# A twelfth block by seven products in the MLPs of a two-layer decoder: block 13 joins, and three moves that go with it

## The chip, the cores and the metric

The kernel runs on one core of a Trainium2 chip, as one program. Its metric is the device time in microseconds (us). The engines of the core are TensorE (PE, with its weight loads, PEld), VectorE (DVE), ScalarE (ACT), GpSimd (POOL) and SyncE (SP, which only issues transfers). Each takes its own instructions strictly in the order in which the program wrote them, and they meet through semaphores alone.

## The reference: what is computed

Two decoder layers over 256 tokens of 1024 numbers, all in float32. Each layer is an attention (stick-breaking in the first, native sparse in the second) and an MLP with a residual, and a last norm follows. The change is in the MLP, called twice, and in the last norm:

```
def sqrelu_mlp(x, w1, w2):
    h = jax.nn.relu(x @ w1)
    return (h * h) @ w2

h = h + sqrelu_mlp(rms_norm(h, norm_gain[layer, 1]), mlp_w1[layer], mlp_w2[layer])
...
return rms_norm(h, final_norm)      # x * rsqrt(mean(x * x) + eps) * gain
```

w1 is 1024 x 4096, w2 is 4096 x 1024.

## The kernel before, in words

**Precision.** A float32 product is made of three matmuls (`mm3`): both operands are split into a high part (rounded by a cast) and a low part (the rest), and high x high, high x low and low x high are added up in PSUM. The split is two instructions per operand: a cast on ScalarE makes the high part, a subtraction on VectorE the low part. In the profile wh and wl are the parts of weights, hh and hl those of the hidden numbers, th and tl those of sums of weights.

**Blocks.** The MLP's 4096 hidden numbers are worked off in 16 blocks of 256 (`NFC`), numbered 0 to 15. For block c, `first` (L651 on) computes the hidden numbers in two halves of 128 for all 256 tokens (pu, 16 matmuls each), each into a bank of PSUM, which ScalarE copies to SBUF (mu, L674). `square` (L678 on) adds the two partial results (L689), applies relu and square on ScalarE (L690, L691) and splits them (L695, L696). `half`, called twice per block, multiplies block c - 2 by its piece of w2. That piece is a 2 x 2 arrangement of 128 x 512 tiles, as the hidden numbers are 2 x 2 (two halves of tokens, two halves of hidden numbers). The plain way needs eight products of tiles, which is 24 matmuls.

**Seven products.** Blocks in `FAST` do it with seven products, 21 matmuls, as Strassen's and Winograd's method does. Five products run on sums or differences of tiles. The sums of hidden numbers are made on VectorE (L705 to L707, with a split of 1024 instead of 512 + 256 elements). The two sums of weight tiles are made in one of four buffers (`four0`, `four2` and the two halves of `fours`), into which the block's w2 is loaded: item b by an accumulating transfer that GpSimd issues (L394: the DMA adds what it reads from HBM to what stands in SBUF) and two additions on VectorE (L420, L423), then item a by a second accumulating transfer. They give th and tl (L372, L437). Item a's transfer is queued when b's first addition is done. A buffer is loaded anew when both sums of its last block are split; the count over the four buffers runs on from the first layer to the second.

**Accumulators.** The products go to seven accumulators in PSUM, numbered 1 to 7. Accumulators 2, 3, 4 and 5 end as the four quarters of the result (two halves of tokens t, two halves of columns n), while 1, 6 and 7 hold the products that several quarters share. `gather` combines 1, 6 and 7 (copies on ScalarE, L745 and L746; sums on VectorE, L747 and L748) and adds them to the residual `hres` (`res`, L585), scaled by the norm's factor. Before the change this runs when block 12 is done, while block 15's hidden numbers are computed. Blocks 14 and 15 are multiplied last, quarter by quarter in a given `order`, so that each quarter can be finished while the next is computed; `mid` then calls what follows: in the first layer the turning of the result for the next projection (`to_nsa`: matmuls against the identity, L499), in the second `finish`, the last norm, in which the very last quarter is split into two pieces of 256 columns.

**The order.** Nothing reorders at run time. While the program is written, a planner (`Order`) simulates ScalarE, VectorE and GpSimd with a cost for each operation. Chains of operations (`go`, with a rank) wait for their predecessors in simulated time, and whatever is ready with the lowest rank is written next into its engine's queue. `need` moves the simulated time on to the end of a chain that TensorE depends on. For an accumulating transfer the planner reckons an end (`add_by_queue`, L390 on): the issue plus 1100 and 2700 ns, or behind the transfers before it, plus a fixed mark. Loads are written for SP by `fetch`, in the order of `feed_mlp`, as their buffers come free. `closing` (L1671 on) loads the last norm's gains (gf) and scales them on ScalarE (`whole`, L1677); `gain` (L1712) multiplies a finished quarter by them.

Of the kernel before, what the change touches and what calls it, by code (L numbers as in the profile page):

```python
# [25 lines left out]
NFC = 16  # L26
NGN = 6
EVAC = (0,)
R_GELU, R_SCT, R_SOFT = 0.7, 0.85, 0.9
FAST = ((2, 3, 4, 5, 6, 7, 8, 9, 10, 11, 12),) * 2  # L30
EPS = 1e-5
NEG = -1e30
GELU_C = 2.0 * 0.7978845608028654
# [127 lines left out]
def act(n, f, more=0):  # L161
    return {"A": (195 + 0.835 * n + more, f, False)}


def dve(n, f, more=0, port=False):
    return {"D": (150 + 1.045 * n + more, f, port)}
# [7 lines left out]
def hybrid_kernel(ctx, tc, x, xt, eye, gcols, gfin, wqk, wv, wo0, wkv, wvs, wq, wg, wo1, w1, w2, cw1, cw2, cpos, gate_b, consts, out):  # L174
    nc = tc.nc
# [7 lines left out]
    o = Order()  # L183

    def go(gen, rank=1, lag=LAG):
        return Chain(o, gen, rank, o.now + lag)
# [12 lines left out]
    def B(i, name, dt=F32):  # L199
        return ps.tile([P, 512], dt, tag=f"b{i}", name=name, bufs=1)  # L200
# [26 lines left out]
    def feed_mlp(layer):  # L227
        first = [[feed(w1[layer, c][:, h * H:(h + 1) * H], H) for c in range(2)] for h in range(2)]
        wa, wb = [[first[h][c] for h in range(2)] for c in range(2)], []

        def one(c, h):
            wa[c].append(feed(w1[layer, c][:, h * H:(h + 1) * H], H))

        def two(c, wide):
            s = [w2[layer, c][:, h * H:(h + 1) * H] for h in range(2)]
            fast = c in FAST[layer]
            x = feed(s[0], H, own="x" if fast else False)
            if fast:
                loads.append((s[1], H, 1, "y"))
                ls = [len(loads) - 2, len(loads) - 1]  # L240
                y = item("w", 512, ls[1:])
                quads.append(ls)
            if wide:
                one(c + 2, 1)
            if fast:
                b = item("b", H, ls)
                wb.append([x, y, item("a", H, ls), b])
                pairs[b] = pairs[wb[-1][2]] = x, y
            else:
                wb.append([x, feed(s[1], H)])  # L250

        for c in range(2, NFC):
            wa.append([])
            one(c, 0)
            if not 4 <= c < NFC - 1:
                one(c, 1)
            two(c - 2, 4 <= c < NFC - 1)
        for c in (NFC - 2, NFC - 1):
            two(c, False)
        return wa, wb  # L260
# [22 lines left out]
    class Weights:  # L283
        raws, lands, gone, cur, path, extra, pool, open, four = [], [], 0, -1, 0.0, 0.0, None, False, None

    ws = Weights()
# [103 lines left out]
    def add_by_queue(to, other):  # L390
        w = Waiter()

        def issue():
            nc.gpsimd.dma_start(to, other, accum_op=OP.add)  # L394
            ws.path = max(ws.path, o.t + 1100) + 1450
            ws.extra = max(ws.extra, o.t + 1100) + 2700
            o.at(max(ws.path, ws.extra) + 4300, w.finish)
        return {"G": (1300, issue, False)}, w

    def sums(i, p):  # L400
# [179 lines left out]
    def res(n, t, a, r=None, c0=0, c1=512):  # L580
        hv = hres[t][:, n * 512 + c0:n * 512 + c1]
        if r is None:
            yield dve(512, lambda: nc.vector.tensor_add(hv, a, hv))
        else:
            yield dve(c1 - c0, lambda: nc.vector.scalar_tensor_tensor(hv, a[:, c0:c1], r, hv, op0=OP.mult, op1=OP.add), 60)  # L585
# [11 lines left out]
    def mlp(layer, gi, x_, ch, pt, rs, pus, accs, extra, mid, order, ends, late, ap):  # L597
# [8 lines left out]
        wa, wb = i_m[layer]  # L606
        fast = FAST[layer]
        acc = {}
        banks = {"z": pus[0][0], 1: extra[0], 2: accs[0], 3: accs[2], 4: accs[1], 5: accs[3], 6: extra[1], 7: extra[2]}
        held = []  # L610
        r2, rn = [None, None], [None, None]
        A11, A21, A12, A22, E2, S3, S1, Q, S4 = range(9)

        def term(m, hT, a, w, n, last=False, q=(0, 512)):
            o.need(hT[2][a > 3])
            new = m not in acc
            if new:
                acc[m] = B(banks[m], f"acc{m}")
            a = hT[3][a] * P
            b = cut(W(w), n * 512 + q[0], n * 512 + q[1])  # L620
            mm3(acc[m][:, q[0]:q[1]], (hT[0][:, a:a + P], hT[1][:, a:a + P]), b, new, last)
# [29 lines left out]
        def first(c, st, f, k0, k1):  # L651
            pu, (u, s), chains = st
            if k0 == 0 and c >= 4:
                if free[0] is not None:
                    o.need(free[0])
                pu[f] = B(extra[2] if f and c == NFC - 1 else pus[1][1], "pu")
            for part in range(2):
                for k in range(k0, k1):
                    if c < 2:
                        w, col = W(wa[c][k // 4]), k % 4 * 256 + f * P  # L660
                        if part == 0:
                            o.need(ch[k])
                    else:
                        w, col = W(wa[c][f]), k * P
                    a = cut(w, col, col + P)
                    if part == 0:
                        mm(pu[f], a[0], x_[2][:, k, :, :], k == 0, False)
                    else:
                        mm(pu[f][:, 0:T * P], a[1], x_[0][:, k, :], False, k == NK - 1)
            if c >= 2:  # L670
                gone(wa[c][f])
            if k1 == NK:
                def gen():
                    yield act(512, lambda: nc.scalar.copy(u[:, f, :], pu[f]))  # L674
                chains.append(go(gen(), 0.3))
                free[0] = chains[-1]
# [65 lines left out]
        def gather():  # L742
            g = slot(2, [P, 2, 512], F32, "gp")
            p, v = g[:, 0], g[:, 1]
            yield act(512, lambda: nc.scalar.copy(v, acc[7]))  # L745
            yield act(512, lambda: nc.scalar.copy(p, acc[1]))  # L746
            yield dve(512, lambda: nc.vector.tensor_sub(p, p, acc[6]))  # L747
            yield dve(512, lambda: nc.vector.tensor_add(v, v, p), port=True)  # L748
            yield from res(0, 0, acc[1], r2[0])
            yield from res(1, 0, p, rn[0])  # L750
            yield from res(0, 1, v, r2[1])
            yield from res(1, 1, v, rn[1])

        gathered = None
        for c in range(2, NFC):
            if c == 5:
                scaled = go(scales(), 3)
            st = begin(c)
            apart = 4 <= c < NFC - 1
            first(c, st, 0, 0, NK)  # L760
            if apart:
                half(*held[0], 0)
            first(c, st, 1, 0, NK)
            held.append((c, square(c, st)))
            if not apart:
                half(*held[0], 0)
            half(*held.pop(0), 1)
            if c - 2 == fast[-1]:
                o.need(scaled)
                gathered = go(gather(), 1.5)  # L770
                ws.four = None
                late()

        o.need(gathered)
        for i, (t, n) in enumerate(order):
            m = {(0, 0): 2, (1, 0): 4, (0, 1): 3, (1, 1): 5}[t, n]
            pair = {2: ((A11, 0, 0), (A12, 1, 0)), 4: ((A21, 0, 0), (A22, 1, 0)),
                    5: ((A22, 0, 1), (A21, 1, 1)), 3: ((E2, 0, 1), (S3, 1, 1))}[m]
            for a, h, nn in pair:
                term(m, held[0][1], a, wb[held[0][0]][h], nn)  # L780
            if len(ends[i]) > 1:
                early = go(res(n, t, acc[m], r2[t], *ends[i][0]), 0.19)
            for q in ends[i]:
                if q[0]:
                    o.need(early)
                for a, h, nn in pair:
                    term("z" if q[1] < 512 else m, held[1][1], a, wb[held[1][0]][h], nn, h == 1, q)
                c = [go(res(n, t, acc["z"] if q[1] < 512 else acc[m], r2[t], *q), 0.2)]
                if m == 5:
                    also = go(res(1, 0, acc[m], r2[0]), 0.21)  # L790
                mid(i, t, n, q, c + ([also] if m == 3 else []))
        for h in held:
            gone(wb[h[0]])

# [871 lines left out]
    fin = {}  # L1666
# [4 lines left out]
    def closing():  # L1671
        fin["gf"] = gf = slot(0, [P, D], F32, "gf")
        fin["ys"] = wide_slot(0, [P, T, 2, D], F32, "ys")
        nc.sync.dma_start(gf, gfin.to_broadcast([P, D]))

        def whole():
            yield {"A": (290 + 0.84 * D, lambda: nc.scalar.activation(gf, gf, AF.Copy, scale=float(D) ** 0.5), False)}  # L1677
        go(whole(), 3, 9000)

    def finish(i, t, n, q, c):  # L1680
        gf, ys = fin["gf"], fin["ys"]
# [2 lines left out]
        h = slice(n * 512, (n + 1) * 512)  # L1684
        g = slice((1 - n) * 512, (2 - n) * 512)
        q = slice(n * 512 + q[0], n * 512 + q[1])
        m = q.stop - q.start
# [21 lines left out]
            (nc.scalar if late else nc.sync).dma_start(out[t * P:(t + 1) * P, r], y[:, r])  # L1709

        def gain():
            yield dve(512, lambda: nc.vector.tensor_mul(y[:, h], hres[t][:, h], gf[:, h]), port=True)  # L1712

        def gen():
# [139 lines left out]
```

## Time and profile before

| | |
|---|---|
| time, median of 3 runs | 600.11 us (599.98 to 600.43) |
| the profiled execution's own time | 600.43 us |
| its span, first to last instruction | 598.7 us |
| TensorE busy | 588.6 us, 98% of the span |
| VectorE busy | 515.6 us, 86% |
| ScalarE busy | 433.0 us, 72% |
| GpSimd busy | 94.2 us, 16% |
| mean granted clock of TensorE | 0.997 |

The profile is of one execution. Starts of instructions are in us from the first instruction, and busy is the time in which an engine has an instruction in work. A line's "idle before" is how long its engine had nothing in work before it, with the one that ended the wait. Matmuls are pipelined: one of 512 columns lasts some 390 ns, while the next begins about 230 ns behind it, so stretches, not durations, are summed on TensorE. Most instructions of VectorE and ScalarE also begin a little before the one ahead has ended.

### The profile page before, as it was taken

To read this page: it belongs to the slowest core of one execution; us is meant where nothing else is said; L and a number is where in the kernel's file an instruction comes from. 1 tells how busy PE (TensorE), PEld (TensorE's weight loads), DVE (VectorE), ACT (ScalarE), POOL (GpSimd) and SP (SyncE) were. 2 spreads that over 40 slices of the span, in tenths; PEclk is the share of its full clock that TensorE was granted. 3 is DMA by queue.
4 is the path that set the end of the run, shared out by engine and by line. 5 is a ranking of instruction groups with operands and counts; after the bars stand their busy time and mean duration, and the time that the engine had idled before them with its cause. 6 is when DMAs were issued, how large, how long until landed. Compare 5 with 4: busy or idle time off the path is not lost.

```text
span 598.7 us, 9366 instructions
## 1 busy us (share of the span) xinstructions
PE 588.6 (98%) x3352; PEld 493.1 (82%) x3352; DVE 515.6 (86%) x828; ACT 433.0 (72%) x705; POOL 94.2 (16%) x111
## 2 busy tenths in 40 slices
PE   9999999999999999999999999999999999899995
PEld 6888888888888888888897888777888888688884
DVE  6788997689999999986876899964989999799965
ACT  6767667587988879875925795663878887688863
POOL 0013330001212120000120435130011111111000
PEclk9999999999999999999999999999999999999998
DMA  8982434389987995555553635303699878884502
GB/s 323 401 300 89 133 129 152 108 314 363 244 259 234 248 279 132 153 192 182 176 177 141 249 105 177 107 17 124 197 399 305 229 202 258 240 232 136 158 1 71
DMA packets 37630, 118.78 MB, mean 198 GB/s; under 512 B 4560, under 2 KB 6096, under 8 KB 37584
## 3 DMA queue, kind: packets, MB, share of 16 engines
q1 hardware_dynamic: 31248, 106.88, 50.6%
q0 software_dynamic: 5760, 10.49, 10.7%
q10 hardware_dynamic: 576, 0.82, 0.4%
q8 instruction: 26, 0.43, 0.3%
q14 instruction: 20, 0.16, 0.1%
HBM read 117.12 MB, written 1.05 MB: 197 GB/s over the span
## 4 chain that ended last, share of the span: by engine, by line
PE 86%; ACT 6%; DMA 4%; DVE 2%; issue 1%; POOL 0%; ACTq 0%; POOLq 0%; DVEq 0%
PE acc L487 30%; PE pu L487 26%; PE qk L487 8%; PE pk L487 4%; PE pv L487 4%; PE po L487 3%; PE qp L487 3%; PE z L487 2%; ACT wh L372 2%; DMA fours<-in_w 2%; ACT pe L1341 2%; PE ptp L499 1%; DMA raw<-in_w 1%; PE ph L487 1%; PE pt L499 1%; PE pa L499 1%
## 5 line engine op out<-in xcount | busy, mean ns | idle before, releaser
L387 DVE TENSOR_TENSOR wl<-raw,wh 128x1024 fp32r<-128x1024 f32 x136 | 168.0, 1252 | 7.7 <-ACT wh L372 7.2
L372 ACT CAST wh<-raw 128x1024 fp32r<-128x1024 f32 x136 | 140.7, 1051 | 30.0 <-DMA raw<-in_wq 8.3
L487 PE MATMUL pu<-xn,wh 128*128 128x512 f32 x512 | 128.8, 391 | 0.6 <-ACT mu L674 0.6
L487 PEld LDWEIGHTS pu<-xn,wh 128*128 128x128 f32 x512 | 94.5, 188 | 20.0 <-ACT mu L674 1.4
L487 PEld LDWEIGHTS pu<-xn,wl 128*128 128x128 f32 x512 | 70.9, 190 | 5.7
L487 PE MATMUL pu<-xn,wl 128*128 128x256 f32 x512 | 72.6, 282 | 0.0
L487 PE MATMUL acc<-wh,hh 128*128 128x512 f32 (+1 forms) x146 | 57.1, 391 | 0.0
L487 PE MATMUL acc<-wl,hh 128*128 128x512 f32 (+1 forms) x146 | 56.9, 390 | 0.0
L487 PE MATMUL acc<-wh,hl 128*128 128x512 f32 (+1 forms) x146 | 56.6, 388 | 0.0
L394 POOL DMA_DIRECT2D four<-in_w x22 | 20.5, 932 | 182.5 <-ACT wh L372 61.8
L674 ACT COPY mu<-pu 128x512 f32<-128x512 f32 x64 | 37.3, 582 | 8.7 <-PE pu L487 8.5
L487 PE MATMUL acc<-wh,oT 128*128 128x512 f32 x128 | 43.3, 401 | 0.0
L696 DVE TENSOR_TENSOR hl<-ms,hh 128x1024 fp32r<-128x1024 f32 (+2 forms) x42 | 37.2, 901 | 1.7 <-ACT hh L695 1.5
L487 PE MATMUL acc<-tl,hh 128*128 128x512 f32 x88 | 34.6, 393 | 0.8 <-DVE tl L437 0.8
L487 PE MATMUL acc<-th,hh 128*128 128x512 f32 x88 | 34.6, 394 | 0.3 <-ACT th L372 0.3
L695 ACT CAST hh<-ms 128x1024 fp32r<-128x1024 f32 (+2 forms) x42 | 32.9, 795 | 2.7 <-DVE ms L707 2.3
L487 PE MATMUL acc<-th,hl 128*128 128x512 f32 x88 | 34.2, 389 | 0.0
L487 PE MATMUL pk<-wh,xk 128*128 128x512 f32 (+1 forms) x128 | 32.9, 340 | 0.0
L1341 ACT ACTIVATE pe<-pe,nm 128x256 f32<-128x256 f32 (+1 forms) x64 | 28.4, 447 | 5.6 <-DVE nm L1339 5.6
L487 PE MATMUL qk<-xa,wh 128*128 128x512 f32 x128 | 32.5, 395 | 0.0
L487 PEld LDWEIGHTS acc<-wh,hl 128*128 128x128 f32 x146 | 27.4, 188 | 5.8
L437 DVE TENSOR_TENSOR tl<-four,th 128x1024 fp32r<-128x1024 f32 x24 | 29.1, 1218 | 3.4 <-ACT th L372 3.3
(230 smaller groups left out, 1189.0 us busy)
## 6 DMA issues: line engine op xcount, KB each, us to landing
raw<-in_w SPq DMA_DIRECT2D x84, 512.0 KB, 5.5
four<-in_w SPq DMA_DIRECT2D x24, 512.0 KB, 7.8
fours<-in_w SPq DMA_DIRECT2D x20, 512.0 KB, 7.6
raw<-in_wqk SPq DMA_DIRECT2D x16, 512.0 KB, 6.2
raw<-in_wo SPq DMA_DIRECT2D x16, 512.0 KB, 3.9
four<-in_w POOLq DMA_DIRECT2D x22, 256.0 KB, 5.7
fours<-in_w POOLq DMA_DIRECT2D x18, 256.0 KB, 7.1
raw<-in_wkv SPq DMA_DIRECT2D x8, 512.0 KB, 4.0
```

The lines of the kernel that those rows point to most:

```text
L372: k = {"A": (195 + 0.835 * m, lambda: nc.scalar.copy(a, b), False), "D": (200 + 0.49 * m, lambda: nc.vector.tensor_copy(a, b), True)}
L387: yield {"D": (150 + 1.045 * m, lambda: nc.vector.tensor_sub(lo, raw, f32(hi)), True)}
L394: nc.gpsimd.dma_start(to, other, accum_op=OP.add)
L437: yield {"D": (150 + 1.045 * H, lambda: nc.vector.tensor_sub(lo2, both, f32(hi2)), True)}
L487: nc.tensor.matmul(o_, a, b, start=first, stop=last, skip_group_check=True)
L499: nc.tensor.transpose(o_, a, i)
L674: yield act(512, lambda: nc.scalar.copy(u[:, f, :], pu[f]))
L695: yield act((b - a) * P, lambda: nc.scalar.copy(hh[:, into], flat[:, q]))
L696: yield dve((b - a) * P, lambda: nc.vector.tensor_sub(hl[:, into], flat[:, q], f32(hh[:, into])), port=True)
L1341: act(n, lambda: nc.scalar.activation(d, d, AF.Exp, bias=nm[:, i:i + 1], scale=-1.0, accum_out=rs[:, t, hd, b:b + 1]), 150)]
```

## The change

Block 13 joins the blocks with seven products, in both layers (`FAST` is now blocks 2 to 13 of 0 to 15), which gives each layer twelve such blocks and 24 sums of weight tiles. Blocks 4 to 15 now all have their first `half` put between the two halves of their hidden numbers; before, block 15's two hidden halves ran one behind the other, with the second in the bank of accumulator 7, which was free by then. The load of the second half of block 15's first-layer weights comes behind block 13's.

The accumulators 1, 6 and 7 are now complete only behind block 13, which is the last block ahead of the closing order. So `gather` starts there, with rank 0.25 in place of 1.5 and accumulator 1 added to the residual first. The products of block 14 for the first two quarters come before anything of block 15 (`pair_of`). The first two quarters' later steps wait for `gather`; `need(gathered)` stands before the third quarter's later steps, and in the last round before its last pieces, one of which takes accumulator 1's bank in the second layer.

The planner's fixed mark for the end of an accumulating transfer goes from 4300 to 5800 ns. `closing` is called with `gather`, one block later; its scaling has rank 1 and a lag of 4000 ns in place of rank 3 and 9000, and `gain` now waits for it in the plan.

```diff
-FAST = ((2, 3, 4, 5, 6, 7, 8, 9, 10, 11, 12),) * 2
+FAST = (tuple(range(2, 14)),) * 2
...
             one(c, 0)
-            if not 4 <= c < NFC - 1:
+            if c < 4:
                 one(c, 1)
-            two(c - 2, 4 <= c < NFC - 1)
+            two(c - 2, c >= 4)
...
-            o.at(max(ws.path, ws.extra) + 4300, w.finish)
+            o.at(max(ws.path, ws.extra) + 5800, w.finish)
...
-                pu[f] = B(extra[2] if f and c == NFC - 1 else pus[1][1], "pu")
+                pu[f] = B(pus[1][1], "pu")
...
             p, v = g[:, 0], g[:, 1]
-            yield act(512, lambda: nc.scalar.copy(v, acc[7]))
+            yield from res(0, 0, acc[1], r2[0])
             yield act(512, lambda: nc.scalar.copy(p, acc[1]))
-            yield dve(512, lambda: nc.vector.tensor_sub(p, p, acc[6]))
+            yield [dve(512, lambda: nc.vector.tensor_sub(p, p, acc[6])), act(512, lambda: nc.scalar.copy(v, acc[7]))]
             yield dve(512, lambda: nc.vector.tensor_add(v, v, p), port=True)
-            yield from res(0, 0, acc[1], r2[0])
             yield from res(1, 0, p, rn[0])
...
-            apart = 4 <= c < NFC - 1
+            apart = c >= 4
...
-                gathered = go(gather(), 1.5)
+                gathered = go(gather(), 0.25)
...
-        o.need(gathered)
+        pairs_of = {2: ((A11, 0, 0), (A12, 1, 0)), 4: ((A21, 0, 0), (A22, 1, 0)),
+                    5: ((A22, 0, 1), (A21, 1, 1)), 3: ((E2, 0, 1), (S3, 1, 1))}
+        m_of = [{(0, 0): 2, (1, 0): 4, (0, 1): 3, (1, 1): 5}[x] for x in order]
+
+        def pair_of(j):
+            for a, h, nn in pairs_of[m_of[j]]:
+                term(m_of[j], held[0][1], a, wb[held[0][0]][h], nn)
+
         for i, (t, n) in enumerate(order):
-            m = {(0, 0): 2, (1, 0): 4, (0, 1): 3, (1, 1): 5}[t, n]
-            pair = {2: ((A11, 0, 0), (A12, 1, 0)), 4: ((A21, 0, 0), (A22, 1, 0)),
-                    5: ((A22, 0, 1), (A21, 1, 1)), 3: ((E2, 0, 1), (S3, 1, 1))}[m]
-            for a, h, nn in pair:
-                term(m, held[0][1], a, wb[held[0][0]][h], nn)
+            m = m_of[i]
+            pair = pairs_of[m]
+            if i != 1:
+                pair_of(i)
+            if i == 0:
+                pair_of(1)
+            if i == 3:
+                o.need(gathered)
...
-                mid(i, t, n, q, c + ([also] if m == 3 else []))
+                if i == 2:
+                    o.need(gathered)
+                mid(i, t, n, q, c + ([also] if m == 3 else []) + ([gathered] if i < 2 else []))
...
-        go(whole(), 3, 9000)
+        fin["whole"] = go(whole(), 1, 4000)
...
         def gain():
+            yield fin["whole"]
             yield dve(512, lambda: nc.vector.tensor_mul(y[:, h], hres[t][:, h], gf[:, h]), port=True)
```

## The prediction

> **What bounds the kernel now.** I read the page first, for what is busy.
>
> ```profile
> span 598.7 us, 9366 instructions
> ...
> PE 588.6 (98%) x3352; PEld 493.1 (82%) x3352; DVE 515.6 (86%) x828; ACT 433.0 (72%) x705; POOL 94.2 (16%) x111
> ```
>
> TensorE sets the time: 588.6 of 598.7 us. So a matmul fewer is time saved, as long as nobody makes TensorE wait. Whether somebody does is read by stage. The second view is a table of stretches (length, then busy time and count of PE, weight loads, DVE, ACT, POOL; then clock, DMA share, GB/s). It covers blocks 4 to 13 of the second MLP: five blocks, one, another, three.
>
> ```profile
> 453.01:504.58 51.57, 51.57 (x266) 44.14 (x265) 50.17 (x71) 44.15 (x58) 8.74 (x10) 1.00 0.83 242
> 504.58:517.40 12.82, 11.10 (x55) 8.60 (x53) 9.44 (x12) 7.96 (x11) 1.75 (x2) 1.00 0.83 211
> ...
> 528.04:559.09 31.05, 31.05 (x161) 26.59 (x160) 30.95 (x41) 26.40 (x35) 3.52 (x4) 1.00 0.59 172
> ```
>
> Two things are to be seen. A block takes 10.35 us (31.05/3) with TensorE full, and one block takes 12.82: 2.47 us are lost there. And VectorE is nearly as full as TensorE, 30.95 of 31.05: work that the change adds to VectorE has little room beside the matmuls.
>
> Third, the timelines about the lost 2.47 us (start, length, instruction, idle time before and who ended it): ScalarE, then TensorE, then GpSimd.
>
> ```profile
> 512.97 1.05 ACT L372 CAST th<-four 128x1024 fp32r<-128x1024 f32 x1 [3.55 <-DMA four<-in_w]
> ```
>
> ```profile
> 514.07 0.51 PE L487 MATMUL acc<-th,hh 128*128 128x512 f32 x1 [0.34 <-ACT th L372]
> 515.33 0.51 PE L487 MATMUL acc<-tl,hh 128*128 128x512 f32 x1 [0.76 <-DVE tl L437]
> ...
> 517.40 2.12 PE L487 MATMUL pu<-xn,wh 128*128 128x512 f32 x8 [0.63 <-ACT mu L674]
> ```
>
> ```profile
> 502.26 0.88 POOL L394 DMA_DIRECT2D fours<-in_w  x1 [12.32 <-DVE hl L696]
> 502.95 1.09 POOL L394 DMA_DIRECT2D four<-in_w  x1
> ```
>
> A cast of summed weights (th) stands in ScalarE's queue 3.55 us for an accumulating transfer into "four". GpSimd issued it at 502.95, directly behind another one that had kept its queue waiting. It landed just before 512.97, some 10 us later. All transfers of this kind together, with who waited for them:
>
> ```profile
> who waited for it (us, times):
>   ACT th L372: 6.1, 4
> ...
> DMA to landing us min/median/max: 4.1/6.2/10.8
> ```
>
> **The change, part by part.** *Block 13 by seven products.* The chain of waits lists TensorE's stretches in order (start, length, count). First a plain block (both halves), then the two halves of a fast one; then, for use below, the end of the first MLP.
>
> ```profile
> 141.79 5.47 PE acc L487 x24
> ...
> 150.02 2.07 PE acc L487 x9
> ...
> 154.85 2.75 PE acc L487 x12
> ...
> 266.88 13.63 PE acc L487 x60
> 280.51 0.87 PE pt L499 x8
> ```
>
> 24 matmuls take 5.47 us, 21 take 2.07 + 2.75 = 4.82. Block 13 changes from the one to the other in each of two layers: 2 x 0.65 = **1.30 us less on TensorE**, which is the path.
>
> What it adds elsewhere is read from VectorE's timeline, a fast block's rows first, a plain block's after.
>
> ```profile
> 548.44 1.22 DVE L437 TENSOR_TENSOR tl<-four,th 128x1024 fp32r<-128x1024 f32 x1
> 549.58 1.22 DVE L387 TENSOR_TENSOR wl<-four,wh 128x1024 fp32r<-128x1024 f32 x1
> 550.71 0.41 DVE L705 TENSOR_TENSOR ms<-ms 128x256 f32<-128x256 f32 x1
> 551.05 0.68 DVE L420 TENSOR_TENSOR four<-four 128x512 f32<-128x512 f32 x1
> 551.65 0.28 DVE L706 TENSOR_TENSOR ms<-ms 128x128 f32<-128x128 f32 x1
> ...
> 553.19 0.68 DVE L387 TENSOR_TENSOR wl<-four,wh 128x512 fp32r<-128x512 f32 x1
> 553.91 0.69 DVE L423 TENSOR_TENSOR four<-four 128x512 f32<-128x512 f32 x1
> 554.51 1.22 DVE L696 TENSOR_TENSOR hl<-ms,hh 128x1024 fp32r<-128x1024 f32 x1
> ...
> 558.52 2.35 DVE L387 TENSOR_TENSOR wl<-raw,wh 128x1024 fp32r<-128x1024 f32 x2
> 560.79 0.42 DVE L710 TENSOR_TENSOR ms<-ms 128x256 f32<-128x256 f32 x1
> 561.13 1.22 DVE L437 TENSOR_TENSOR tl<-four,th 128x1024 fp32r<-128x1024 f32 x1
> 562.27 1.02 DVE L696 TENSOR_TENSOR hl<-ms,hh 128x512 fp32r<-128x512 f32 x2
> ```
>
> A fast block's weights take 1.22 + 0.68 (wl), 0.68 + 0.69 (sums) and 2 x 1.22 (tl) = 5.71 us, its hidden part 0.41 + 2 x 0.28 (L706, and L707 like it) + 1.22 = 2.19: together 7.90. A plain block takes 2.35 + 0.42 + 1.02 = 3.79. So VectorE gets 4.1 us more per layer. What hides it is how far ahead VectorE is by then: the tl at 561.13 ends at 562.35, and TensorE first uses it here:
>
> ```profile
> 568.14 0.39 PE L487 MATMUL acc<-tl,hh 128*128 128x512 f32 x1
> ```
>
> That is 5.8 us early, and it is block 12's last. Block 13's sums take the next place in the line, due one block of 10.35 us later. A fast block needs 7.90, plus 0.68 for the hidden sum and 2 x 1.22 for the next first-layer weights: 11.0 us of VectorE in 10.35, so the lead shrinks by about 0.7 to 5. Cost on the path: nothing; if that lead were gone, up to 2 x 4.1 us. In the second layer VectorE also gets back what it stood idle in the stall (12.82 - 9.44 = 3.4 us).
>
> ScalarE's added casts:
>
> ```profile
> 549.76 1.04 ACT L372 CAST th<-four 128x1024 fp32r<-128x1024 f32 x1
> 550.70 0.61 ACT L372 CAST wh<-four 128x512 fp32r<-128x512 f32 x1
> ```
>
> Two th casts more, and one whole cast (taken at 1.04 too) becomes 0.61: + 1.65 us per layer. ScalarE has 31.05 - 26.40 = 4.65 us free in three blocks, so this is hidden. GpSimd gets two more issues per layer of about 1 us each and is 16% busy, but its queue is in order: an issue that waits for a load holds the one behind it, as at 502.26.
>
> *Order of loads and banks for block 15.* The load of the second half of its first-layer weights moves behind block 13's two loads in SP's queue. SP was through with its loads here, when it issued the next thing, the last norm's factors:
>
> ```profile
> 561.33 0.38 SPq L1674 DMA_DIRECT2D gf<-in_gfin  x1
> ```
>
> Block 15 begins only at 559.09 + 10.35 = 569.4, so this costs nothing. The factors are still queued behind the last load, wherever the text now calls for them: they are there long before the first product with them. That product now waits for the scaled factors by name: nothing. Block 15's second hidden bank is now the common one. Its copy to SBUF hides under the 2.07 us half that is put between.
>
> *Accumulators combined behind block 13.* The combining (two copies, six VectorE steps) ran under block 15; here its first copy in the second layer, and its last step:
>
> ```profile
> 569.47 0.59 ACT L745 COPY gp<-acc 128x512 f32<-128x512 f32 x1 [2.16 <-PE acc L487]
> ```
>
> ```profile
> 578.43 0.75 DVE L585 SCALAR_TENSOR_TENSOR hres<-gp,rn,hres 128x512 f32<-128x512 f32 x1
> ```
>
> It took 9.7 us, at low rank between other work. The new place begins after block 13's last matmul. In the first layer the turning matmuls (280.51) need all of it: between lie six groups of six matmuls, 36 x 13.63/60 = 8.2 us. Its bare steps are, by these rows, 0.59 for a copy, 2 x 0.69 for the sums and 4 x 0.75, about 5.0 us; with a higher rank they give way less. So it costs between 0 and 9.7 - 8.2 = 1.5 us. In the second layer the squares and gains of the first two outputs now wait for it and pile up near the end: again 0 to 1.5. There is room for both:
>
> ```profile
> 579.20:591.60 12.40, 12.37 (x60) 10.22 (x58) 7.57 (x15) 4.09 (x11) 0.56 (x1) 1.00 0.00 0
> 271.10:280.51 9.41, 9.41 (x44) 7.76 (x43) 5.11 (x7) 2.76 (x5) 1.19 (x3) 1.00 0.73 233
> ```
>
> VectorE is idle for 4.8 and 4.3 us there, as much as the combining needs. I take + 0.2 in each layer, near the low end.
>
> *Later order behind accumulating transfers.* The planner's mark for the end of such a transfer moves 1.5 us back: it reckoned 1.1 + 2.7 + 4.3 = 8.1 us from the issue, now 9.6. The longest took 10.8. This adds no instruction; it puts other ready casts and subtractions ahead of th and tl. In the stall, order alone can save only what stood behind the th: the 0.63 us wait for mu and something of the rest. The 0.34 + 0.76 us are the late landing itself. But the order, GpSimd's queue and the buffers' rotation (22 sums before, 24 now, over four buffers, so that the second layer starts in another one) all shift, and the stall was a coincidence in one of the nine blocks shown. Bounds: 0 (it comes again) to 2.47 saved; a cost too, below. I take **2.0 saved**, nearer to the rows of the eight full blocks.
>
> By the Trainium skill, "DMA: Bandwidth & Descriptors", section on the anatomy of one DMA on the SWDGE path, a GpSimd-issued DMA takes about 2.0 us plus its bytes over 436 GB/s: 2.6 us for 256 KB, an estimate. By that the old mark was already late enough, and a later one can gain nothing: 599.2, the first rival's time. The trace disagrees on the size, 4.1 to 10.8.
>
> *Sum.* The profiled execution took 600.43 us (span 598.7 and 1.7 around it), the highest of three and 0.32 above their median of 600.11. 600.43 - 1.30 - 2.0 + 0.4 = 597.5, and 597.2 against the median.
>
> **Rivals.** *The stall stays.* The late landing comes from GpSimd's queue order and a slow load, which the change doesn't mend. Then 600.11 - 1.30 + 0.4 = 599.2. For it: 1.10 us of the stall is the landing. Against it: everything in the second layer shifts.
>
> *The combining comes too late.* With 1.5 us in each layer in place of 0.2: 597.2 - 0.4 + 3.0 = 599.8. For it: it took 9.7 us before. Against: its rank, and VectorE's idle time.
>
> *The later mark makes the transfers themselves late, and it is slower.* The second sum's transfer is only put in GpSimd's queue once the first sum is made, and that is now planned up to 1.5 us later, so it may also fall behind the next block's. ScalarE stood waiting for a transfer at four places. If each lands 1.5 us later, that is at most 6.0 us; with half of it taken up by the lead and the old stall kept, 600.11 - 1.30 + 3.0 = 601.8. It decides where a landing comes later than 1.05 + 1.22 = 2.3 us (th, tl) before its matmul. Against it: the other sums have more lead, like the 5.8 us above.
>
> **How the numbers follow.** The forecast has 0.58, the stall that stays 0.20, the late combining 0.10, the late transfers 0.12. 0.2% is 1.2 us, about what a measurement of this kernel can tell from no change: faster is below 598.9, slower above 601.3. The forecast is faster but for 0.01; a stall that stays in part is faster (0.07) or the same (0.13); late combining is mostly the same (0.07), with 0.02 faster and 0.01 slower; late transfers are slower (0.10) or the same (0.02). So faster 0.66, same 0.23, slower 0.11. The range goes from 595.8 (all 2.47 us saved, no cost at the ends, 596.3, and half a microsecond of scatter in other waits) to 601.2, which leaves out most of the last rival.
>
> **What would show it.** TensorE with 3346 matmuls, six fewer. Blocks 12 and 13 at 10.35 us each, with no wait of TensorE for tl. Accumulators' first VectorE step right behind block 13, the last one before the transposes in layer 0, with no idle time ahead of those. No TensorE gap over 0.3 us in blocks 4 to 13 of layer 1, and ScalarE's wait for accumulating transfers well below 6.1 us. The forecast is wrong if such a gap is there again, if VectorE's lead over TensorE is used up before block 13, or if the tail behind the last matmul grows from its 7 us.

## The result, and the profile after

The kernel went from 600.05 us (median of four executions, 599.39 to 600.43) to **596.51 us** (four executions, 596.19 to 597.56): a ratio of 0.9945, with a 95% interval of 0.9928 to 0.9962. That is 3.54 us less. The profiled execution of the changed kernel is its slowest, 597.56 us, as that of the kernel before was (600.43), so the two traces differ by 2.87 us and not by 3.54.

The page of the changed kernel, busy time by engine:

```profile
span 595.8 us, 9379 instructions
...
PE 586.3 (98%) x3346; PEld 492.2 (83%) x3346; DVE 522.5 (88%) x838; ACT 437.5 (73%) x707; POOL 98.0 (16%) x115
```

Six matmuls fewer, 6.9 us more busy time on VectorE, 4.5 more on ScalarE, and TensorE still has 98% of the span. The table of stretches for the second MLP of the changed kernel (length, then busy time and count of PE, weight loads, DVE, ACT, POOL; clock, DMA share, GB/s): eight blocks from block 4 on, then one, then two.

```profile
452.08:534.84 82.76, 82.76 (x426) 70.85 (x425) 80.16 (x110) 70.84 (x91) 14.02 (x16) 1.00 0.85 250
534.84:546.22 11.38, 10.36 (x54) 8.53 (x52) 9.02 (x12) 7.53 (x11) 1.74 (x2) 1.00 0.75 182
546.22:567.23 21.01, 21.01 (x107) 17.98 (x108) 20.87 (x28) 18.19 (x23) 1.73 (x2) 1.00 0.45 126
```

Eight blocks take 82.76/8 = 10.35 us each, as full blocks did before. One still stalls: 11.38 in place of 12.82. ScalarE's and TensorE's timelines of the changed kernel show it as the old stall, smaller and three blocks later, a cast of th that waits for an accumulating transfer:

```profile
540.85 1.05 ACT L372 CAST th<-four 128x1024 fp32r<-128x1024 f32 x1 [2.61 <-DMA four<-in_w]
...
545.60 0.57 ACT L674 COPY mu<-pu 128x512 f32<-128x512 f32 x1
```

```profile
546.22 2.14 PE L487 MATMUL pu<-xn,wh 128*128 128x512 f32 x8 [1.02 <-ACT mu L674]
```

What is late for TensorE is no longer th. It is mu, the copy that empties a bank: it stands behind this th and four other casts in ScalarE's queue. All accumulating transfers of the changed kernel (before: 6.1 us, four times; 4.1/6.2/10.8):

```profile
who waited for it (us, times):
  ACT th L372: 3.4, 2
...
DMA to landing us min/median/max: 4.1/6.5/10.3
```

The transfers land no sooner than before. They are waited for less.

Cut at the same five places, by the starts of TensorE's instructions in each profiled execution, the spans differ as follows (us). "A" is blocks 4 to 14 of the first MLP, "B" goes from its block 15 to block 4 of the second MLP, "C" is blocks 4 to 14 of the second, "D" goes on to the last matmul's end, "E" is what lies behind. Eleven full blocks take 113.81. The rows below the first two are experiments. One execution of e5_changed took 729.75 us at a granted clock of 0.752 and is left out of its figures.

| kernel | A | B | C | D | E |
|---|---|---|---|---|---|
| before | 114.07 | 191.69 | 116.42 | 22.30 | 7.09 |
| after | 113.83 | 190.99 | 115.15 | 21.58 | 7.13 |
| e1_no_block13 | 113.81 | 193.16 | 113.81 | 22.29 | 7.09 |
| e2_mark_4300 | 113.84 | 190.99 | 116.33 | 21.58 | 7.13 |
| e3_before_mark_5800 | 113.87 | 192.37 | 113.81 | 22.29 | 7.09 |
| e4_gather_late | 113.88 | 191.03 | 113.81 | 21.59 | 7.13 |
| e5_changed | 113.81 | 191.14 | 113.81 | 21.58 | 7.13 |
| e6_before_mark_second | 113.83 | 191.69 | 113.81 | 22.29 | 7.09 |
| e7_block13_first_only | 113.83 | 191.00 | 113.81 | 22.29 | 6.63 |
| e8_before_b_later | 113.84 | 191.73 | 113.81 | 22.29 | 6.93 |
| e9_gains_gpsimd | 113.88 | 191.01 | 113.83 | 21.59 | 6.66 |
| e10_mark_2800_second | 113.83 | 191.03 | 116.40 | 21.59 | 7.14 |
| e11_gains_and_b_later | 113.90 | 191.32 | 113.86 | 21.58 | 6.66 |
| e12_changed_again | 113.87 | 191.03 | 113.83 | 21.58 | 7.13 |

Of the 2.87 us between the two traces, B and D give 0.70 + 0.72 = 1.42, C gives 1.27, A gives 0.24 (a small wait less in the first MLP), and E takes 0.04.

### The profile page after: what moved, and what is told of

It reads as the page before. It is cut to its first block, busy times and chain, and to the rows that moved or that the text cites. A ratio compares the mean times of both kernels' runs of the same rounds, so it can differ in the third digit from the quotient of the medians.

```text
span 595.8 us, 9379 instructions
## 1 busy us (share of the span) xinstructions
PE 586.3 (98%) x3346; PEld 492.2 (83%) x3346; DVE 522.5 (88%) x838; ACT 437.5 (73%) x707; POOL 98.0 (16%) x115
## 4 chain that ended last, share of the span: by engine, by line
PE 86%; DMA 5%; ACT 5%; DVE 2%; issue 1%; SPq 0%; ACTq 0%; POOL 0%; POOLq 0%
PE acc L487 31%; PE pu L487 27%; PE qk L487 8%; PE pk L487 4%; PE po L487 3%; PE qp L487 3%; PE pv L487 3%; PE z L487 2%; DMA four<-in_w 2%; ACT wh L372 2%; ACT pe L1352 2%; DMA fours<-in_w 2%; PE ptp L499 1%; DMA rv<-in_wv 1%; PE ph L487 1%; PE pt L499 1%
## 5 line engine op out<-in xcount | busy, mean ns | idle before, releaser
L387 DVE TENSOR_TENSOR wl<-raw,wh 128x1024 fp32r<-128x1024 f32 x132 | 163.3, 1254 | 10.2 <-ACT wh L372 9.8
L372 ACT CAST wh<-raw 128x1024 fp32r<-128x1024 f32 x132 | 135.6, 1051 | 27.7 <-DMA raw<-in_wq 8.8
L487 PE MATMUL acc<-wh,hh 128*128 128x512 f32 (+1 forms) x136 | 53.3, 392 | 0.0
L487 PE MATMUL acc<-wl,hh 128*128 128x512 f32 (+1 forms) x136 | 53.1, 390 | 0.0
L487 PE MATMUL acc<-wh,hl 128*128 128x512 f32 (+1 forms) x136 | 52.7, 388 | 0.0
L394 POOL DMA_DIRECT2D fours<-in_w x24 | 21.5, 895 | 144.0 <-DVE ms L707 57.5
L394 POOL DMA_DIRECT2D four<-in_w x20 | 19.2, 961 | 148.1 <-DMA four<-in_w 61.0
L487 PE MATMUL acc<-th,hh 128*128 128x512 f32 x96 | 37.7, 392 | 0.0
L487 PE MATMUL acc<-tl,hh 128*128 128x512 f32 x96 | 37.6, 392 | 0.0
L487 PE MATMUL acc<-th,hl 128*128 128x512 f32 x96 | 37.3, 389 | 0.0
```

Of the source, the lines that this page charges most:

```text
L372: k = {"A": (195 + 0.835 * m, lambda: nc.scalar.copy(a, b), False), "D": (200 + 0.49 * m, lambda: nc.vector.tensor_copy(a, b), True)}
L387: yield {"D": (150 + 1.045 * m, lambda: nc.vector.tensor_sub(lo, raw, f32(hi)), True)}
L487: nc.tensor.matmul(o_, a, b, start=first, stop=last, skip_group_check=True)
```

## The experiments

The theory was the prediction's: 1.3 us from the matmuls, the rest from the stall, by the later mark. The rivals were that something else removes the stall (the rotation of the buffers, or chance), and that the combining costs more or less than it was given. The experiments ran in three later series, on the chips numbered 12 and 5; for the first pair no chip is on record. In these series the kernel before has a median of 598.2 to 598.3, with executions from 597.3 to 601.5. So each is read against the runs of the kernel before beside it, and its stages in the table above.

**Block 13 as before, all else changed (e1_no_block13)**

```diff
-FAST = (tuple(range(2, 14)),) * 2
+FAST = (tuple(range(2, 13)),) * 2
```

> The changed kernel with block 13 by eight products again (11 blocks per layer as before); the later mark, the rank of the combining and the reordered last products stay. My theory (block 13 gives its matmuls, the later mark gives the rest by easing the stall of the second layer): 1.3 us over the changed kernel, about 597.8, and the block that lost 2.47 us before loses about 1 us at most. Rival (the stall moved because the four buffers start elsewhere in the second layer, the mark does nothing): the buffers start as before, so the stall is back and the time is 599 to 600.

Measured: 599.56 us, a ratio of 1.0017 (1.0006 to 1.0027) to the kernel before. In the table D is 0.71 above the changed kernel's, as 3 matmuls should be, but B is 2.17 above. The surplus is new waits, in stages that the edit doesn't mean. ScalarE's timeline of e1_no_block13 at the end of the first MLP, then TensorE's:

```profile
272.00 1.05 ACT L372 CAST wh<-raw 128x1024 fp32r<-128x1024 f32 x1 [2.16 <-PE acc L487]
272.96 0.63 ACT L690 ACTIVATE ms<-ms 128x512 f32<-128x512 f32 x1
```

```profile
274.95 0.50 PE L487 MATMUL acc<-wh,hh 128*128 128x512 f32 x1 [0.27 <-ACT hh L695]
...
380.13 0.66 PE L499 MATMUL ptp<-ident,pe 128*128 128x128 f32 x4 [0.41 <-ACT pT L1405]
```

A cast for the next stage stands ahead of block 15's relu and waits 2.16 us for a buffer; and in the attention behind, a turning matmul waits. These two gaps are 0.68 us of the 1.47 by which B exceeds that of the kernel before; the rest was not traced. The planner's order is one for the whole program: an edit in one stage moves others, and the medians of such kernels are not the price of the edit. What this run does show is in C: with the old rotation of 22 sums and the mark at 5800 there is no stall in this trace, 113.81. So the time lies in the rival's 599 to 600, but not by the rival's mechanism.

**The changed kernel with the old mark (e2_mark_4300), and the reverse (e3_before_mark_5800)**

```diff
-            o.at(max(ws.path, ws.extra) + 5800, w.finish)
+            o.at(max(ws.path, ws.extra) + 4300, w.finish)
```

> The changed kernel with the planner's old mark of 4300. Theory: the stall comes back in the second layer, 598.3 to 599.0 (2 us over the changed kernel). Rival (buffers): no different from the changed kernel, 596.2 to 597.

> The kernel before with the mark at 5800 and nothing else. Theory: the mark alone gives about 2 us, 598, with ScalarE's 3.55 us wait in front of a th cast at least halved. Rival (buffers, or chance of the whole order): within 0.5 us of the kernel before, 599.6 to 600.4, the wait as long.

Measured: e2_mark_4300 596.95 us, ratio 0.9974 (0.9961 to 0.9988); e3_before_mark_5800 598.50, ratio 0.9997 (0.9986 to 1.0008). By the medians the mark does next to nothing, on either kernel, as the rival had it for e2_mark_4300. By the one trace of each it does all: C is 116.33 with the new rotation and the old mark, 113.81 with the old rotation and the new mark. ScalarE's timeline of e2_mark_4300:

```profile
510.95 1.05 ACT L372 CAST th<-four 128x1024 fp32r<-128x1024 f32 x1 [2.23 <-DMA four<-in_w]
...
539.09 1.05 ACT L372 CAST th<-four 128x1024 fp32r<-128x1024 f32 x1 [1.33 <-DMA four<-in_w]
...
551.24 1.05 ACT L372 CAST th<-four 128x1024 fp32r<-128x1024 f32 x1 [2.96 <-DMA four<-in_w]
```

Both are right. The profiled execution of e2_mark_4300 is its slowest, 599.34; ten of its other eleven are between 596.18 and 597.30. The stall comes in some executions and not in others.

The changed kernel itself shows this. The runs after, e5_changed and e12_changed_again are one program, with the same instructions in the same order on VectorE, ScalarE and GpSimd, and C is 115.15, 113.81 and 113.83. GpSimd's two accumulating transfers in front of the stall, in the changed kernel and then in e12_changed_again, each pair with its time to landing:

```profile
529.76 0.88 POOL L394 DMA_DIRECT2D fours<-in_w  x1 [7.38 <-DVE tl L437]
530.46 1.07 POOL L394 DMA_DIRECT2D four<-in_w  x1
...
DMA to landing us min/median/max: 8.4/9.4/10.3
```

```profile
528.90 0.87 POOL L394 DMA_DIRECT2D fours<-in_w  x1 [7.43 <-DVE ms L707]
529.60 1.07 POOL L394 DMA_DIRECT2D four<-in_w  x1
...
DMA to landing us min/median/max: 5.1/6.7/8.3
```

The order is the same, the landings are not: the load in front of the first transfer took 9.45 us in the one and 8.16 in the other, the second transfer 10.3 and 8.3, and ScalarE waited 2.61 us for it or not at all.

And e3_before_mark_5800 also has waits of its own in B, 192.37 against 191.69 (its turning matmul at 379.96 us waits 0.42 us, like that of e1_no_block13), which hide what the mark saves. That needed an edit that leaves the first layer alone.

**The mark in the second MLP alone, in the kernel before (e6_before_mark_second)**

```diff
-            o.at(max(ws.path, ws.extra) + 4300, w.finish)
+            o.at(max(ws.path, ws.extra) + ws.mark, w.finish)
...
-        ws.tp = ap
+        ws.tp, ws.mark = ap, (4300, 5800)[layer]
```

> The kernel before with the later mark in the second MLP only, so that everything up to there is written in the old order. Theory (the mark takes the stall away): no gap of TensorE over 0.3 us in the second MLP, the times lie close together, and the median is that of the stall-free executions, 597.3 to 598.0 on a chip whose floor is 597.3. Rival (the mark does nothing, the order of the attention cost e3 0.7 us by itself): a spread as wide as the kernel before's and its median within 0.3 us.

Measured: 598.18 us (597.51 to 598.90 in 12 executions), a ratio of 0.9989 (0.9976 to 1.0002). The kernel before beside it: 598.34, 597.29 to 601.45. The stretch C of e6_before_mark_second:

```profile
453.28:567.09 113.81, 113.81 (x584) 97.45 (x583) 110.33 (x146) 95.62 (x123) 15.83 (x18) 1.00 0.77 219
```

TensorE is busy for the whole of it, and B, D and E are those of the kernel before. In these 12 executions the upper end of the times, which reached 601.45, is gone, as the theory had it. The median moves by 0.16 only, as the rival had it, and the interval of the ratio includes 1.

**The mark still earlier, in the changed kernel's second MLP (e10_mark_2800_second)**

```diff
-            o.at(max(ws.path, ws.extra) + 5800, w.finish)
+            o.at(max(ws.path, ws.extra) + ws.mark, w.finish)
...
-        ws.tp = ap
+        ws.tp, ws.mark = ap, (5800, 2800)[layer]
```

> The changed kernel with the mark moved the other way, to 2800, in the second MLP only. Theory (an early mark puts casts ahead of their transfers): longer and more waits of ScalarE in front of th casts than with 4300 (2.2, 1.3 and 3.0 us in e2's profile), blocks 4 to 14 of the second MLP above 115.5 us in place of 113.8, and a median over 597.5. Rival (the mark only shuffles the order): no worse than the changed kernel, 596.3 to 597.

Measured: 598.72 us (597.58 to 601.69), against 596.65 (596.01 to 597.03) for the changed kernel on the same chip, e12_changed_again: 2.07 us slower. The waits for accumulating transfers in the second MLP, and three of the casts in ScalarE's timeline of e10_mark_2800_second:

```profile
who waited for it (us, times):
  ACT th L372: 7.6, 7
...
DMA to landing us min/median/max: 4.2/6.0/8.9
```

```profile
486.55 1.05 ACT L372 CAST th<-fours 128x1024 fp32r<-128x1024 f32 x1 [2.35 <-DMA fours<-in_w]
...
518.00 1.05 ACT L372 CAST th<-fours 128x1024 fp32r<-128x1024 f32 x1 [3.00 <-DMA fours<-in_w]
...
538.62 1.05 ACT L372 CAST th<-four 128x1024 fp32r<-128x1024 f32 x1 [1.02 <-DMA four<-in_w]
```

With the rotation and everything else kept, an earlier mark gives seven waits in place of none to two in the other traces of the changed kernel, although no transfer here took more than 8.9 us. So the mark sets how often th stands ahead of its transfer, and that is not a matter of buffers.

**The first transfer later in GpSimd's queue, in the kernel before (e8_before_b_later).** In the old stall two accumulating transfers stood behind each other in GpSimd's queue. The loads into that buffer, which SP issued from 489.88 on, in the kernel before:

```profile
489.88 0.87 SPq L320 DMA_DIRECT2D fours<-in_w  x2
...
DMA to landing us min/median/max: 8.9/10.1/11.3
```

The second one, issued at 490.3, landed 11.3 us later, at 501.6. Only then could GpSimd issue item b's transfer (502.26), and item a's, for which th was to wait, came behind it (502.95). The profile's row names a VectorE instruction as the releaser of that wait, which ended within 0.1 us of the load. But the issue comes 0.66 to 0.67 us behind the landing of that block's load in four traces (this one, e6_before_mark_second, and the pairs of the changed kernel and of e12_changed_again above), and 0.18 to 0.58 behind the instruction that is named: it is the load that was waited for. The edit lets item b's chain start later in the plan, in the second layer, with the mark at 4300:

```diff
-... got[min(p, cuts - 1)] + (1500 if kind in "ab" else 0))
+... got[min(p, cuts - 1)] + (1500 if kind == "a" else ws.hold if kind == "b" else 0))
...
-        ws.tp = ap
+        ws.tp, ws.hold = ap, (1500, 5000)[layer]
```

> The kernel before with the first accumulating transfer of a block (b) put into GpSimd's queue 3.5 us later in the plan, in the second MLP only, so that it no longer stands ahead of the second transfer (a) of the block before while its load is still under way. Theory of the queue (a late load of b holds up a): no idle time of ScalarE over 1 us in front of a th cast, and 597.3 to 598.0 on a chip whose floor is 597.3. Rival (the transfer itself is slow, wherever it stands): waits and times as in the kernel before.

Measured: 597.88 us (597.19 to 598.80), a ratio of 0.9986 (0.9973 to 0.9999). GpSimd's timeline of e8_before_b_later at the same place, then its stretch C:

```profile
497.97 0.88 POOL L394 DMA_DIRECT2D four<-in_w  x1 [8.01 <-ACT mu L674]
498.51 1.25 POOL L394 DMA_DIRECT2D fours<-in_w  x1
```

```profile
453.00:566.81 113.81, 113.81 (x584) 97.44 (x583) 110.90 (x146) 95.59 (x123) 15.88 (x18) 1.00 0.77 220
```

Item a's transfer now stands first, 0.54 us ahead of b's, and the stall is gone from the trace, with the old mark: ScalarE waits for no accumulating transfer in the second MLP. But the trace doesn't show that the order did it. The load that took 11.3 us before took 7.9 here (issued at 489.36, landed at 497.26), so that in the old order too item a's transfer would have gone out near 498.5, an estimate from GpSimd's second row, in place of 502.95. It is the same in e6_before_mark_second. There the load took 7.7 us, and the two transfers stand in the old order:

```profile
499.18 0.88 POOL L394 DMA_DIRECT2D fours<-in_w  x1 [9.37 <-DVE ms L707]
499.87 1.09 POOL L394 DMA_DIRECT2D four<-in_w  x1
```

So no trace shows what either edit does when a load is late. That they help is read from the times: none of the 24 executions of the two took more than 598.90 us, while 8 of the 31 of the kernel before beside them took 599.29 or more. That those 8 had the stall is inferred, as none of them has a trace. Nor is it settled whether GpSimd's order or ScalarE's is what helps: both edits put other casts first in ScalarE's queue as well, and no kernel here changes one queue alone.

**The combining at its old rank (e4_gather_late)**

```diff
-                gathered = go(gather(), 0.25)
+                gathered = go(gather(), 1.5)
```

> The changed kernel with the combining at the old rank of 1.5. My theory: VectorE has room, so 596.5 to 597.2, and the turning matmuls in the first layer wait 0 to 0.5 us. Rival (late combining): it takes 9.7 us as before, the turning matmuls wait 1.5 us and the last layer's end grows by as much: 598.5 to 599.5.

Measured: 597.01 us, a ratio of 0.9969 (0.9957 to 0.9982); B 191.03, D 21.59 and E 7.13 are the changed kernel's to 0.04. The rank costs nothing in either layer's stretches. The median can't be told from the changed kernel's on that chip, 596.65 in another series (e12_changed_again).

**Block 13 in the first layer alone (e7_block13_first_only)**

```diff
-FAST = (tuple(range(2, 14)),) * 2
+FAST = (tuple(range(2, 14)), tuple(range(2, 13)))
```

> The changed kernel as it is, timed with the next three beside the same kernel before. Where the accounts agree: 1.3 us under the kernel before from the matmuls. Theory that the stall is a matter of chance from one execution to the next: where the kernel before has it in few executions (median near its lowest), the whole gain is 1.3 to 1.8 us; where it has it in most, 3 to 3.6 us.

> The changed kernel with block 13 by eight products in the second MLP only; the first MLP and the attention stay as changed. Theory (three matmuls are worth 0.65 us per layer and nothing else hangs on them): 0.65 us over the changed kernel. Rival (VectorE bears the added sums only just, they cost TensorE something): less than 0.4 us over it, or under it.

Measured on one chip: the changed kernel again (e5_changed) 596.60, ratio 0.9961 (0.9947 to 0.9975); e7_block13_first_only 596.85, ratio 0.9965 (0.9951 to 0.9978). Block 13's second-layer part was expected to be worth 0.65 us and is worth 0.25. The table says why: against e5_changed D is 0.71 longer, as three matmuls are, but E is 0.50 shorter. So in the second layer the later combining costs half a microsecond behind the last matmul. VectorE's timeline at the end of the changed kernel, whose last matmul ends at 588.65; then TensorE's last one into accz:

```profile
587.72 0.68 DVE L1724 TENSOR_TENSOR ys<-hres,gf 128x512 f32<-128x512 f32 x1
588.32 0.48 DVE L585 SCALAR_TENSOR_TENSOR hres<-accz,r,hres 128x256 f32<-128x256 f32 x1
588.71 0.48 DVE L585 SCALAR_TENSOR_TENSOR hres<-acc,r,hres 128x256 f32<-128x256 f32 x1
```

```profile
587.52 0.28 PE L487 MATMUL accz<-wh,hl 128*128 128x256 f32 x1
```

accz is complete at 587.80, but a product with the norm's gains, put off by the combining, stands ahead in VectorE's queue: the residual of accz starts 0.52 us late. In the kernel before it started 0.04 behind its matmul.

**Those products on GpSimd (e9_gains_gpsimd), with the later b as well (e11_gains_and_b_later), and the changed kernel beside them (e12_changed_again)**

```diff
-            yield dve(512, lambda: nc.vector.tensor_mul(y[:, h], hres[t][:, h], gf[:, h]), port=True)
+            yield pool(512, lambda: nc.gpsimd.tensor_mul(y[:, h], hres[t][:, h], gf[:, h]))
```

> The changed kernel with the products of the finished quarters and the last norm's gains on GpSimd in place of VectorE. Theory (at the end VectorE makes a gain product of 0.68 us ahead of the next to last residual piece, because the combining came late, and the chain behind the last matmul starts 0.5 us later): that piece starts 0.8 us before the last matmul's end as in the kernel before, the last store lands 0.5 us sooner behind the last matmul (5.55 against 6.05 us), and the time is 0.3 to 0.5 us under the changed kernel. Rival (the end hangs on ScalarE's squares or on the stores): no different.

> The changed kernel with both: the gains on GpSimd and the first accumulating transfer of a block put 3.5 us later into GpSimd's queue in the second MLP. Theory: 0.5 us from the end and what is left of the stall (about 0.2 us in the mean, the spread's upper end): 595.6 to 596.2, and no execution over 597. Rival (with the later mark the queue no longer matters): the same as the gains alone.

> The changed kernel once more, as the measure of the three beside it on the same chip: 596.3 to 597.0 where the kernel before has its median near 598.3, 596.5 where that is at 600.

Measured: e9_gains_gpsimd 596.12 us, ratio 0.9962 (0.9947 to 0.9977); e11_gains_and_b_later 596.29, ratio 0.9963 (0.9949 to 0.9977); e12_changed_again 596.65, ratio 0.9971 (0.9960 to 0.9981). VectorE at the end of e9_gains_gpsimd (last matmul's end 587.44), then GpSimd:

```profile
586.32 0.20 DVE L1737 TENSOR_SCALAR ssq<-ssq 128x1 f32<-128x1 f32 x1
586.63 0.48 DVE L585 SCALAR_TENSOR_TENSOR hres<-accz,r,hres 128x256 f32<-128x256 f32 x1
587.48 0.48 DVE L585 SCALAR_TENSOR_TENSOR hres<-acc,r,hres 128x256 f32<-128x256 f32 x1 [0.36 <-PE acc L487]
```

```profile
581.38 1.67 POOL L1724 TENSOR_TENSOR ys<-hres,gf 128x512 f32<-128x512 f32 x1 [20.89 <-DVE hres L585]
583.99 2.70 POOL L1724 TENSOR_TENSOR ys<-hres,gf 128x512 f32<-128x512 f32 x2 [0.94 <-DVE hres L585]
```

The residual of accz starts 0.04 us behind its matmul again, E falls from 7.13 to 6.66, and the median by 0.53, though the intervals of the two ratios overlap. The last store lands 5.58 us behind the last matmul, in the changed kernel 6.05. These three products take twice as long on GpSimd, and no instruction waits for them. The later b adds nothing on top: with the later mark no effect of it is to be seen. These two are the fastest kernels of the study.

## Why the prediction was right, and where it was not

**The matmuls: right.** 3346 of them. Predicted 1.30 us less; B and D give 0.70 + 0.72, and between the experiments D differs by 0.70 to 0.72 wherever block 13's second-layer part does.

**VectorE and ScalarE beside it: right.** The lengths of VectorE's instructions add up to 8.0 us more than before, those of ScalarE's to 3.7, near the 2 x 4.1 and 2 x 1.65 of the prediction. No wait for tl or th of block 13 is in the trace. VectorE's lead is seen in its timeline and TensorE's, in the second layer of the changed kernel:

```profile
570.71 1.22 DVE L437 TENSOR_TENSOR tl<-fours,th 128x1024 fp32r<-128x1024 f32 x1
```

```profile
576.28 0.39 PE L487 MATMUL acc<-tl,hh 128*128 128x512 f32 x1
```

It ends at 571.93 and is used 4.35 us later; predicted was "about 5", from 5.8.

**The combining: the sum was near, its parts were not.** Predicted 0.2 in each layer. In the first layer it costs nothing. VectorE's timeline of the changed kernel, its first and last step there, and the chain of waits with the turning matmuls, which wait for nobody:

```profile
271.44 0.74 DVE L585 SCALAR_TENSOR_TENSOR hres<-acc,r,hres 128x512 f32<-128x512 f32 x1
...
277.73 0.74 DVE L585 SCALAR_TENSOR_TENSOR hres<-gp,rn,hres 128x512 f32<-128x512 f32 x1
```

```profile
268.69 10.91 PE acc L487 x48
279.60 0.87 PE pt L499 x8
```

7.0 us of combining in the 8.2 that were there. In the second layer it costs 0.5, not as a wait of TensorE and not where the prediction looked, but behind the last matmul, by the products that it pushes back into VectorE's last microseconds. The prediction had named the pile of "squares and gains of the first two outputs" and priced it by idle time, which does not see that one instruction of 0.68 stands in front of another on the path. In the measured time that cost barely shows against the kernel before: the store lands 0.5 later (6.05 against 5.55 us behind the last matmul), but the span ends 1.08 us behind that landing in place of 1.54, and E grows by 0.04. Why that last piece differs is open.

**The mark: near in size by luck, and wrong in how.** Predicted was 2.0 us of 2.47. The two traces give 1.27 in C and 0.24 in A. In the first series the whole gain was 3.54; taking off the 1.42 of B and D leaves 2.1, which fits a stall that the kernel before had in each of its four executions there, but only one of them has a trace. In two later series the kernel gained 1.74 (e5_changed) and 1.53 (e12_changed_again) by the medians, 2.05 and 1.72 by the means: 0.1 to 0.6 more than the matmuls. Had the first series been like these, 2.0 would have been far too much.

The step that failed is that the prediction took the stall as a fixed amount of the kernel and the landing as given: "order alone can save only what stood behind the th", and "the 0.34 + 0.76 us are the late landing itself". The runs showed a chance of each execution in its place. One program has 115.15 in C once and 113.81 and 113.83 twice, and the late load of 11.3 us took 7.7 and 7.9 in e6_before_mark_second and e8_before_b_later, which lose nothing in C. What the order sets is how often a landing is waited for: seven times with the mark at 2800. And the sum counted for the order only what stood in ScalarE's queue, while in the kernel before item a's transfer had also stood in GpSimd's, behind one that waited for the late load.

The prediction had named a gap of TensorE over 0.3 us in blocks 4 to 13 of the second layer as a sign that it is wrong. The profiled execution of the changed kernel has one, of 1.02 us at 546.22; e5_changed and e12_changed_again have none. Why the first series differs from the others is open.

By the Trainium skill, "DMA: Bandwidth & Descriptors", section on the anatomy of one DMA on the SWDGE path, 256 KB from GpSimd would take 2.6 us, an estimate by its figures, and no mark would matter. Here such transfers took 4.1 to 10.8 us, and with the mark at 2800 the kernel was 2.07 us slower. The measurement decides.

**The sum.** The result is 0.7 us under the forecast of 597.2. The combining took 0.04 of the time in place of 0.4, and the matmuls gave 0.12 more. What is left of the first series' gain, 3.54 - 1.42 + 0.04 = 2.16, is 0.16 more than the mark's 2.0. The last 0.06 is the median before, 600.05 in place of 600.11.

**The rivals.** That the stall stays came true in the profiled execution in a weaker form: a gap of 1.02 us is left there, none in e5_changed and e12_changed_again. That the later mark makes the transfers late fell: with it no trace has more than two waits for them, 3.4 us together, where the kernel before has four, 6.1 us, and e2_mark_4300 three, 6.5 us. That the combining is late came true by a third of its price, in one layer.

## What to carry to other kernels

Where engines run a written order, plan a transfer to end near the longest that the trace shows, not near its median (here the planned ends of 9.6 and 6.6 us from the issue, with a median of 6.2 and a longest of 10.8 before, were 2.07 us apart), and look at what is queued ahead of it on the engine that issues it. A stall that depends on a late transfer has a chance as well as a size: take several executions, and more than one series, before its removal is counted as a gain. For the last microseconds don't add up idle time: read which instruction stands in front of the one on the path, and move it to an engine that has nothing to do.

## What the runs showed of the hardware

- The same program had its median at 600.05 us in one series (all four executions from 599.39 to 600.43) and at 598.2 to 598.3 in three others (597.29 to 601.45), with a mean granted clock of 0.996 to 0.999 in every trace. The changed kernel has 596.5 to 596.7 in all of its series.
- A load of 512 KB took 11.3 us from its issue to its landing, and the same load 7.7 us in e6_before_mark_second and 7.9 in e8_before_b_later. The difference is a third of a block's 10.35 us, with 0.74 to 0.80 of the DMA engines' time taken in the stretch C of all the runs.
- GpSimd took 1.30 to 1.67 us for a product of 128 x 512 for which VectorE took 0.68. VectorE's own instructions beside it kept their length (0.48 and 0.75).
